# Attention scores of a two-layer diffusion step as sums of three fp32r products, in twelve steps of two heads

## The chip, the core and the metric

The kernel runs on one core of a Trainium2 chip. The metric is the device time of one execution in microseconds (us). The core has a matrix engine (TensorE, PE in the rows, with its weight loads shown apart as PEld), a vector engine (VectorE, DVE), a scalar engine (ScalarE, ACT), GpSimd (POOL) and SyncE (SP), which here only issues DMAs. Each engine works through its own list of instructions in a fixed order and waits on semaphores for the others.

## The reference, cut to what matters

128 context tokens and 256 latent tokens go through two layers of width 1024. A layer is a half-step SwiGLU, a token mixing, and another half-step SwiGLU, each with a norm ahead and behind and modulated by a condition. The mixing projects once and splits the columns among four groups: A (a short gated convolution), B (differential attention), C (a convolution of width 31) and D (grouped-query attention, GQA).

```
def diff_attention(q, k, v, lam):          # 4 heads, 2 maps each, q and k of width 32
        s = jnp.einsum("bqhmd,bshmd->bhmqs", qb, k).astype(jnp.float32) * scale
        p = jax.nn.softmax(s, axis=-1)
        w = p[:, :, 0] - lam * p[:, :, 1]
        return jnp.einsum("bhqs,bshd->bqhd", w.astype(v.dtype), v)
def gqa_attention(q, k, v):                # 4 heads on 2 key heads, width 64
        s = jnp.einsum("bqkgd,bskd->bkgqs", qb, k).astype(jnp.float32) * scale
        p = jax.nn.softmax(s, axis=-1)
        return jnp.einsum("bkgqs,bskd->bqkgd", p.astype(v.dtype), v)
```

Latent tokens attend to 128 cached keys and to the 256 latent ones (384 keys), context tokens to themselves (128 keys). Queries come in three tiles of 128 tokens: t = 0 and 1 latent, t = 2 context. A score product is thus 128 queries by 384 or 128 keys.

## The kernel before, in words

All tokens (3 tiles of 128) stay in SBUF and the weights stream through once. `W` (class at the top) keeps the stream: L156 loads a tile `st` of 128x1024 fp32 on SP's queue, L167 (ACT) casts it to its high half in fp32r, L168 (DVE) subtracts to get the low half; the pair is `wu`. Every large product is a sum of three fp32r products, high·high, high·low and low·high (L542 to L544, L548 to L550 and L576 to L578). Only the small attention products are still plain fp32 matmuls, which the array runs as two passes.

`mix` is the token mixing of one layer. Ahead of the attention it projects group C and D; group C's 31-tap convolution is a chain of 62 multiply-adds on DVE (`conv_some`, L799, tile `cacc`), dealt out a few at a time between other work. Then come 24 attention steps: twelve GQA heads (three query tiles by four heads), then twelve heads of differential attention. Each step is three functions, run one loop pass apart: `first` makes the scores (`probs`: L871 matmul into a PSUM bank `ps_s`, L872 DVE row maximum, L876 ACT exp into `p` with its sum), `second` transposes p (L886) and copies it to `wt` (L888), `third` multiplies with the values (L894, `ps_pv`). A differential head has two maps, joined on DVE (L954, L956, L960). After four heads DVE scales the result into `mo` (L931 or L979). The queries and keys, transposed, lie in `qTd`, `kTd`, `kTdp` (differential) and `qTg`, `kTg`, `kTgp` (GQA), as fp32.

Between the steps run the `fills`, the other projections of the mixing: in the GQA steps `qk_fill` and `v_fill` (for the differential attention, L542 to L544), in the differential steps twelve `a_fill` (group A, L548 to L550, 24 products each) and `norm_fill` (group C's norm, after the convolution). Behind the loop the output projection `ps_o` (L576 to L578) starts with the parts that are done.

The loop, which sets the order of the code:

```
            for i in range(n + 2):
                if i < n:
                    units[i][0]()
                todo = flush()
                run(fills[i])
                run(todo)
                if 1 <= i <= n:
                    units[i - 1][1]()
                if i >= 2:
                    units[i - 2][2]()
                W.tick()
                conv_some(CONV1)
```

`later(f, n)` puts a function off by n passes; `flush` returns those that are due. A scheduler then arranges the instructions of each engine, starting from this order, so an engine's list is near to it but not equal. PSUM has six banks for the large results (`bank`: `ps_j`, `ps_s`, `ps_pv`, `ps_o`) and two for small ones (`mbank`: transposes).

## Time and profile before

| what | value |
|---|---|
| median of 3 runs | 1563.77 us (1561.25 to 1564.76) |
| the profiled execution | 1562.17 us, its span 1560.4 us |
| mean granted TensorE clock | 0.986 of full speed |
| PE busy | 1500.0 us, 96% of the span |
| DVE busy | 1050.7 us, 67% |
| ACT busy | 633.7 us, 41% |
| attention steps, layer 0 | 373.6 to 475.4 us: GQA 51.5 us, differential 50.3 us |
| attention steps, layer 1 | 1130.9 to 1229.8 us: GQA 50.1 us, differential 48.8 us |

Busy shares are means over stages with different limits. PE is busy nearly all the time, but a busy PE may be running small products, or at a lower clock; the granted clock is told per stretch, as a share of full speed. The two attention stretches of a layer are cut where the first score product, the first product of group A and the first product of the output projection start.

### The profile page before, as it was taken

What the parts mean: (1) busy time and instruction counts of PE and PEld (TensorE: products, weight loads), DVE (VectorE), ACT (ScalarE), POOL (GpSimd) and SP (SyncE); (2) the same over time, 40 slices, a digit from 0 to 9 for tenths busy, and PEclk for the clock granted to TensorE, in tenths of its full rate; (3) what the DMA queues carried; (4) which work ended last, traced back from release to release, by engine and by line L of the source; (5) the groups of instructions that cost most, each with busy time, mean ns of one, the idle gap of its engine ahead of it and who ended that gap; (6) DMA issues with size and microseconds to landing.
All of it is one profiled execution on the core that took longest, in us unless ns stands there. A gap on an engine that the chain in (4) does not pass through costs nothing. (4 is left out here: it accounts for less than half of the span.)

```text
span 1560.4 us, 20661 instructions
## 1 busy us (share of the span) xinstructions
PE 1500.0 (96%) x7924; PEld 1319.9 (85%) x7924; DVE 1050.7 (67%) x1454; ACT 633.7 (41%) x1103; POOL 126.4 (8%) x234
## 2 busy tenths in 40 slices
PE   6899999999999999999999999999999999999997
PEld 3699998776887899998879999887768879999885
DVE  3678879867887845677586766984788796333432
ACT  3442233263466632334263333434545764323331
POOL 1101000021001201000021000002100120000000
PEclk9999999998999999999999999999999999999998
DMA  8668767733224555675546656773322245444431
GB/s 307 227 222 261 236 211 236 245 109 98 68 70 145 150 177 179 212 233 172 189 150 215 206 188 200 231 234 110 112 73 92 72 160 175 134 132 138 135 122 41
DMA packets 73619, 260.13 MB, mean 167 GB/s; under 512 B 9728, under 2 KB 9856, under 8 KB 73520
## 3 DMA queue, kind: packets, MB, share of 16 engines
q1 hardware_dynamic: 68112, 246.32, 48.5%
q0 software_dynamic: 4976, 11.70, 2.7%
q8 instruction: 62, 1.02, 0.3%
q10 hardware_dynamic: 432, 0.79, 0.1%
q14 instruction: 37, 0.30, 0.1%
HBM read 256.36 MB, written 2.41 MB: 166 GB/s over the span
## 5 line engine op out<-in xcount | busy, mean ns | idle before, releaser
L168 DVE TENSOR_TENSOR wu<-st,wu 128x1024 fp32r<-128x1024 f32 x322 | 391.6, 1219 | 296.5 <-ACT wu L167 295.9
L167 ACT CAST wu<-st 128x1024 fp32r<-128x1024 f32 x322 | 337.0, 1050 | 585.4 <-DMA st<-ws 253.7
L549 PE MATMUL ps_f<-h,wu 128*128 128x384 f32 x1248 | 418.6, 335 | 0.0
L548 PE MATMUL ps_f<-h,wu 128*128 128x384 f32 x1248 | 418.4, 336 | 0.0
L550 PE MATMUL ps_f<-h,wu 128*128 128x384 f32 x1248 | 418.3, 335 | 0.0
L279 DVE SCALAR_TENSOR_TENSOR acc<-ast,sc,acc 128x1024 f32<-128x1024 f32 x224 | 281.6, 1281 | 27.5 <-DMA ast<-w_ada 26.9
L548 PEld LDWEIGHTS ps_f<-h,wu 128*128 128x128 f32 x1248 | 234.9, 188 | 7.8 <-issue 4.2
L550 PEld LDWEIGHTS ps_f<-h,wu 128*128 128x128 f32 x1248 | 235.0, 188 | 0.0
L549 PEld LDWEIGHTS ps_f<-h,wu 128*128 128x128 f32 x1248 | 235.0, 188 | 0.0
L576 PE MATMUL ps_o<-wu,hid_s 128*128 128x512 f32 x528 | 206.5, 391 | 0.0
L577 PE MATMUL ps_o<-wu,hid_s 128*128 128x512 f32 x528 | 206.0, 390 | 0.0
L578 PE MATMUL ps_o<-wu,hid_s 128*128 128x512 f32 x528 | 205.5, 389 | 0.0
L576 PEld LDWEIGHTS ps_o<-wu,hid_s 128*128 128x128 f32 x528 | 99.1, 188 | 26.1 <-issue 5.9
L578 PEld LDWEIGHTS ps_o<-wu,hid_s 128*128 128x128 f32 x528 | 99.1, 188 | 20.6
L577 PEld LDWEIGHTS ps_o<-wu,hid_s 128*128 128x128 f32 x528 | 99.1, 188 | 20.0
L543 PE MATMUL ps_j<-wu,h 128*128 128x512 f32 (+1 forms) x192 | 73.1, 381 | 5.3 <-DVE wu L168 5.3
L542 PE MATMUL ps_j<-wu,h 128*128 128x512 f32 (+1 forms) x192 | 74.5, 388 | 0.0
L544 PE MATMUL ps_j<-wu,h 128*128 128x512 f32 (+1 forms) x192 | 72.6, 378 | 0.0
L676 ACT ACTIVATE sg<-ps_f 128x384 f32<-128x384 f32 x78 | 38.0, 487 | 83.4 <-PE ps_f L550 79.3
L799 DVE SCALAR_TENSOR_TENSOR cacc<-upad,late,cacc 128x399 f32<-128x399 f32 x120 | 69.9, 630 | 0.0
L337 POOL DMA_DIRECT2D gd<-grow x24 | 11.7, 496 | 676.0 <-DVE grow L329 676.0
L677 DVE TENSOR_TENSOR hid<-sg,ps_f 128x384 f32<-128x384 f32 x78 | 42.9, 549 | 23.3 <-PE ps_f L550 23.3
(234 smaller groups left out, 1701.0 us busy)
## 6 DMA issues: line engine op xcount, KB each, us to landing
st<-ws SPq DMA_DIRECT2D x320, 512.0 KB, 3.9
ast<-w_ada SPq DMA_DIRECT2D x128, 512.0 KB, 4.4
a<-ada SPq DMA_DIRECT2D x16, 512.0 KB, 9.3
G<-gd POOLq DMA_DIRECT2D x12, 512.0 KB, 4.7
brow<-b_ada POOLq DMA_DIRECT2D x24, 64.0 KB, 5.6
prow<-norm_post POOLq DMA_DIRECT2D x24, 64.0 KB, 6.1
x<-x_sample SPq DMA_DIRECT2D x2, 512.0 KB, 5.2
x<-x_prompt SPq DMA_DIRECT2D x1, 512.0 KB, 8.9
```

What stands on the lines that cost most here:

```text
L167: nc.scalar.copy(out=u[:, 0, :], in_=x)
L168: nc.vector.tensor_tensor(out=u[:, 1, :], in0=x, in1=u[:, 0, :].bitcast(F32), op=ALU.subtract)
L279: nc.vector.scalar_tensor_tensor(out=self.acc[c], in0=w, scalar=s1, in1=self.acc[c], op0=ALU.mult, op1=ALU.add)
L542: nc.tensor.matmul(out, lhsT=hk(h, k, 0, tsl), rhs=wh, start=start, stop=False)
L543: nc.tensor.matmul(out, lhsT=hk(h, k, 0, tsl), rhs=wl, start=False, stop=False)
L544: nc.tensor.matmul(out, lhsT=hk(h, k, 1, tsl), rhs=wh, start=False, stop=stop)
L548: nc.tensor.matmul(out, lhsT=wh, rhs=hk(h, k, 0, sl), start=start, stop=False)
L549: nc.tensor.matmul(out, lhsT=wh, rhs=hk(h, k, 1, sl), start=False, stop=False)
L550: nc.tensor.matmul(out, lhsT=wl, rhs=hk(h, k, 0, sl), start=False, stop=stop)
L576: nc.tensor.matmul(out, lhsT=pr[:, 0, s, tsl], rhs=u[:, 0, hsl], start=(q == 0), stop=False)
L577: nc.tensor.matmul(out, lhsT=pr[:, 0, s, tsl], rhs=u[:, 1, hsl], start=False, stop=False)
L578: nc.tensor.matmul(out, lhsT=pr[:, 1, s, tsl], rhs=u[:, 0, hsl], start=False, stop=(q == n - 1))
```

## The change: what it does

1. **Scores as three fp32r products.** The tiles of queries and keys become fp32r with a high and a low half. A helper `halves` writes the high half on ACT (the scaled copy that was there before) and the low half on DVE (one scalar_tensor_tensor, new). The cached keys come in one DMA into `kc` and pass through `halves` too. `probs` gets a list of maps and makes high·high, high·low and low·high of all of them in turn, each map in its own bank.
2. **Twelve steps a layer, of two heads.** A GQA step has two maps, in rows 0 to 63 and 64 to 127 of the array; a differential step has four maps, in four groups of 32 rows.
3. **The order around the steps.** All lags are one pass; in a pass the first fill runs, then `third` of two steps back, then what was put off, then the other fills, then `second`. Weight ticks (two) and convolution taps (8 for 4) per pass are doubled, `a_fill`s come two per step from step 6, `norm_fill`s at steps 8, 9 and 10.
4. **Room.** p gets 6 buffers for 4, `mo` one for 2, the convolution tiles (`c3`) 3 for 4 with `upad` and `zT` sharing a place of their own. `norm_fill` keeps its transposed result in SBUF rather than in three large banks, and the silu at the end is two instructions of 384 rather than six of 128. The tiles `ast` for the condition's weights move from a pool of the whole kernel into each SwiGLU; `sink` and `sc` shrink, `grow` is written in place.

```
-QK_LAG = 2
+QK_LAG = 1
-MIX_LAG = 3
-NORM_LAG = 2
-NORM_AT = 16
-NORM_GAP = 2
+MIX_LAG = 1
+NORM_LAG = 1
+NORM_AT = 8
-CONV1 = 4
-A_STEPS = 11
+CONV1 = 8
...
-        with tc.tile_pool(name=nm("fp"), bufs=1) as fp:
+        with tc.tile_pool(name=nm("fp"), bufs=1) as fp, tc.tile_pool(name=nm("adap"), bufs=2) as ap_:
...
+            kc = mp.tile([P, TOK], F32, tag="p", name=nm("kc"), bufs=6)
+            nc.gpsimd.dma_start(out=kc.rearrange("p (c n) -> p c n", c=3), in_=a["cache_kT"][l])
+
+            def halves(hi, lo, src, scale=1.0):
+                nc.scalar.mul(hi, src, scale)
+                nc.vector.scalar_tensor_tensor(
+                    out=lo, in0=src, scalar=scale, in1=hi.bitcast(F32), op0=ALU.mult, op1=ALU.subtract
+                )
...
-            def probs(t, st, idx, lhsT, rhs):
+            def probs(t, st, maps):
                 nk = TOK if t < 2 else P
-                ps = bank(nm("ps_s"))
-                nc.tensor.matmul(ps[:, 0:nk], lhsT=lhsT, rhs=rhs, start=True, stop=True)
-                nc.vector.tensor_reduce(
...
+                pss = [bank(nm("ps_s")) for _ in maps]
+                for a_, b_ in ((0, 0), (0, 1), (1, 0)):
+                    for ps, (idx, lhsT, rhs) in zip(pss, maps):
+                        nc.tensor.matmul(
+                            ps[:, 0:nk], lhsT=lhsT(a_), rhs=rhs(b_), start=(a_ + b_ == 0), stop=(a_ == 1)
+                        )
+                res = []
+                for ps, (idx, lhsT, rhs) in zip(pss, maps):
+                    nc.vector.tensor_reduce(
...
-                mo = mp.tile([P, 256], F32, tag="mo", name=nm("mo"), bufs=2)
+                mo = mp.tile([P, 256], F32, tag="mo", name=nm("mo"))
...
-                nc.scalar.mul(qTd[:, :, t * P : (t + 1) * P], pq[:, 0:2, :], 32 ** -0.5)
-                nc.scalar.copy(out=kTd[:, :, (t + 1) * P : (t + 2) * P] if t < 2 else kTdp, in_=pq[:, 2:4, :])
+                halves(qTd[:, 0, :, tsl], qTd[:, 1, :, tsl], pq[:, 0:2, :], 32 ** -0.5)
+                k0, k1 = (kTd[:, s, :, ksl] if t < 2 else kTdp[:, s] for s in range(2))
+                halves(k0, k1, pq[:, 2:4, :])
...
-                for hd in range(4)
+                for c in range(2)
...
-                fills[12 + (j * A_STEPS) // 12].append(f)
-            fills[12 + A_STEPS].append(a_split)
+                fills[6 + j // 2].append(f)
+            fills[n].append(a_split)
...
-                run(fills[i])
+                run(fills[i][:1])
+                if i >= 2:
+                    units[i - 2][2]()
                 run(todo)
+                run(fills[i][1:])
                 if 1 <= i <= n:
                     units[i - 1][1]()
-                if i >= 2:
-                    units[i - 2][2]()
-                W.tick()
+                for _ in range(2):
+                    W.tick()
                 conv_some(CONV1)
```

In the lists of the engines this looks as follows (layer 0). The helper lines shift with the edit: L168 of before is L166 of the change, L548 to L550 are L546 to L548, L799 is L803, L871 is L884, L872 is L889, L886 is L904, L894 is L912, L931 is L959; L712 is the low half in `halves`.

PE in the differential half of before: the scores of one head's two maps stand between the products with the values and group A's products.

```order
L886 MATMUL ps_pT_3841<-early,p_3749 128x128 x3
L894 MATMUL ps_pv_3700<-Vd_2812,wt_3804 128x64 x3
L871 MATMUL ps_s_3862<-kTd_2806,qTd_2808 128x384
L871 MATMUL ps_s_3867<-kTd_2806,qTd_2808 128x384
L548 MATMUL ps_j_3828<-h_2555,wu_3495 128x384
L549 MATMUL ps_j_3828<-h_2555,wu_3495 128x384
```

PE at the same place of the changed kernel: twelve score products of four maps stand together, and the products of one map are kept apart by those of the others.

```order
L904 MATMUL ps_pT_3765<-early,p_3623 128x128 x3
L884 MATMUL ps_s_3772<-kTd_2807,qTd_2809 128x384
L884 MATMUL ps_s_3773<-kTd_2807,qTd_2809 128x384
L884 MATMUL ps_s_3774<-kTd_2807,qTd_2809 128x384
L884 MATMUL ps_s_3772<-kTd_2807,qTd_2809 128x384
L884 MATMUL ps_s_3773<-kTd_2807,qTd_2809 128x384
L884 MATMUL ps_s_3775<-kTd_2807,qTd_2809 128x384
L884 MATMUL ps_s_3774<-kTd_2807,qTd_2809 128x384
L884 MATMUL ps_s_3775<-kTd_2807,qTd_2809 128x384
L884 MATMUL ps_s_3772<-kTd_2807,qTd_2809 128x384
L884 MATMUL ps_s_3773<-kTd_2807,qTd_2809 128x384
L884 MATMUL ps_s_3774<-kTd_2807,qTd_2809 128x384
```

PE of the changed kernel at the seam of the two halves, in its first differential step: here the block is broken up by transposes and by the last GQA products with the values (`ps_pv_3482`), and the fourth map `ps_s_3603` stands last, right ahead of group A's products.

```order
L884 MATMUL ps_s_3602<-kTd_2807,qTd_2809 128x384
L904 MATMUL ps_pT_3509<-early,p_3359 128x128 x3
L912 MATMUL ps_pv_3482<-Vg_2815,wt_3507 128x64 x3
L904 MATMUL ps_pT_3583<-early,p_3451 128x128
L912 MATMUL ps_pv_3482<-Vg_2815,wt_3513 128x64 x3
L904 MATMUL ps_pT_3587<-early,p_3454 128x128
L884 MATMUL ps_s_3603<-kTd_2807,qTd_2809 128x384 x3
L546 MATMUL ps_j_3636<-h_2553,wu_3270 128x384
```

DVE of before late in the GQA half: four convolution taps, a row maximum, a weight's low half, and so on.

```order
L799 SCALAR_TENSOR_TENSOR cacc_2936<-upad_2820,late,cacc_2936 128x399 x4
L872 TENSOR_REDUCE st_3418<-ps_s_3419 128x1
L465 TENSOR_TENSOR mTd_3111<-ps_mo_3424,mTd_3111 128x2x128
L168 TENSOR_TENSOR wu_3445<-st_3233,wu_3445 128x1024
L799 SCALAR_TENSOR_TENSOR cacc_2936<-upad_2820,late,cacc_2936 128x399 x4
L872 TENSOR_REDUCE st_3418<-ps_s_3454 128x1
```

DVE of the changed kernel from there to the seam: eight taps stand ahead of a pair of row maxima, the low halves of queries and keys are new, and the row maxima of the first differential step stand behind `mo_3581` and seven more taps.

```order
L803 SCALAR_TENSOR_TENSOR cacc_2937<-upad_2821,late,cacc_2937 128x399 x8
L889 TENSOR_REDUCE st_3441<-ps_s_3442 128x1
L889 TENSOR_REDUCE st_3441<-ps_s_3443 128x1
L712 SCALAR_TENSOR_TENSOR qTd_2809<-ps_qk_3489,qTd_2809 128x2x128
...
L803 SCALAR_TENSOR_TENSOR cacc_2937<-upad_2821,late,cacc_2937 128x399
L959 TENSOR_TENSOR mo_3581<-ps_pv_3482,st_3283 128x256
L803 SCALAR_TENSOR_TENSOR cacc_2937<-upad_2821,late,cacc_2937 128x399 x7
L889 TENSOR_REDUCE st_3599<-ps_s_3600 128x1
```

## Rows read from the trace of the kernel before

**Rows 1.** The page's first lines: the span, and busy time, share of the span and count of instructions of each engine.

```profile
span 1560.4 us, 20661 instructions
PE 1500.0 (96%) x7924; PEld 1319.9 (85%) x7924; DVE 1050.7 (67%) x1454; ACT 633.7 (41%) x1103; POOL 126.4 (8%) x234
```

**Rows 2.** Busy time of each engine (us, with the count) by stretch: the GQA and the differential half of layer 0, then of layer 1. Columns: stretch, its length, PE, PEld, DVE, ACT, POOL, granted clock, DMA share, GB/s.

```profile
373.60:425.10 51.50, 48.88 (x254) 36.98 (x253) 42.23 (x78) 21.97 (x53) 3.54 (x5) 0.90 0.24 78
425.10:475.40 50.30, 49.10 (x290) 41.97 (x289) 39.84 (x103) 31.52 (x81) 5.09 (x10) 0.97 0.21 69
1130.90:1181.00 50.10, 47.46 (x254) 35.97 (x253) 42.18 (x78) 21.93 (x53) 3.54 (x5) 0.93 0.24 81
1181.00:1229.80 48.80, 47.60 (x290) 40.49 (x289) 39.78 (x103) 31.52 (x81) 5.11 (x10) 1.00 0.22 71
```

**Rows 3.** PE's timeline around single score blocks (start us, duration us, then line, operation, tiles; x4 are two maps of two passes each): one of 384 keys in GQA; then of the differential half one in which the maps ran one behind the other in part, one that is split in two, a common one of 384 keys with what stands around it, and one of 128 keys.

```profile
395.64 0.91 PE L871 MATMUL ps_s<-kTg,qTg 64*128 64x384 f32 x2
396.48 0.50 PE L542 MATMUL ps_j<-wu,h 128*128 128x512 f32 x1
...
431.52 1.16 PE L871 MATMUL ps_s<-kTd,qTd 32*128 32x384 f32 x4
...
443.97 0.91 PE L871 MATMUL ps_s<-kTd,qTd 32*128 32x384 f32 x2
...
445.62 0.91 PE L871 MATMUL ps_s<-kTd,qTd 32*128 32x384 f32 x2
...
449.37 0.78 PE L894 MATMUL ps_pv<-Vd,wt 128*128 128x64 f32 x6
450.08 0.91 PE L871 MATMUL ps_s<-kTd,qTd 32*128 32x384 f32 x4
450.93 0.45 PE L548 MATMUL ps_j<-h,wu 128*128 128x384 f32 x1
451.21 0.34 PE L549 MATMUL ps_j<-h,wu 128*128 128x384 f32 x1
451.39 0.35 PE L550 MATMUL ps_j<-h,wu 128*128 128x384 f32 x1
451.57 0.34 PE L548 MATMUL ps_j<-h,wu 128*128 128x384 f32 x1
...
467.98 0.49 PE L871 MATMUL ps_s<-kTdp,qTd 32*128 32x128 f32 x4
468.39 0.45 PE L548 MATMUL ps_j<-h,wu 128*128 128x384 f32 x1
```

**Rows 4.** The same timeline in the first SwiGLU: four fp32 products of 512 columns (eight passes) in four groups of 32 columns of the array, and the product behind them.

```profile
116.90 1.06 PE L291 MATMUL ps_ada<-acc,ones 128*32 128x512 f32 x8
117.90 0.45 PE L548 MATMUL ps_f<-h,wu 128*128 128x384 f32 x1
```

**Rows 5.** DVE's groups by line and shape in the GQA half of layer 0 (373.6 to 425.1 us): count, busy us and mean ns, idle time before them and what ended it.

```profile
L799 DVE SCALAR_TENSOR_TENSOR cacc<-upad,late,cacc 128x399 f32<-128x399 f32 x41 | 23.6, 630 | 0.0
L168 DVE TENSOR_TENSOR wu<-st,wu 128x1024 fp32r<-128x1024 f32 x8 | 9.7, 1219 | 2.8 <-ACT wu L167 2.8
L872 DVE TENSOR_REDUCE st<-ps_s 128x1 f32<-128x384 f32 x8 | 4.4, 554 | 2.6 <-PE ps_s L871 2.6
L872 DVE TENSOR_REDUCE st<-ps_s 128x1 f32<-128x128 f32 x3 | 0.9, 290 | 0.8 <-PE ps_s L871 0.8
...
L820 DVE TENSOR_TENSOR dn<-ps_j,rstd 128x256 f32<-128x256 f32 x1 | 0.4, 424 | 1.5 <-POOL rstd L460 1.5
```

**Rows 6.** The same view of the differential half of layer 0 (425.1 to 475.4 us), four of its groups.

```profile
L872 DVE TENSOR_REDUCE st<-ps_s 128x1 f32<-128x384 f32 x16 | 8.5, 545 | 0.9 <-PE ps_s L871 0.9
L960 DVE SCALAR_TENSOR_TENSOR p<-p,nb,p 128x384 f32<-128x384 f32 x8 | 4.9, 612 | 0.0
L954 DVE RECIPROCAL st<-st 128x2 f32<-128x2 f32 x11 | 1.8, 161 | 3.3 <-ACT p L876 3.3
L960 DVE SCALAR_TENSOR_TENSOR p<-p,nb,p 128x128 f32<-128x128 f32 x2 | 0.7, 345 | 0.0
```

**Rows 7.** PE's waits from the first score product of layer 0 to the end of group C's product (373.6 to 493 us): what waited for what, us in total, times, longest.

```profile
PE ps_j L543 <- DVE wu L168: 2.6, 1, 2.6
PE ps_mo L903 <- DVE mo L994: 0.9, 1, 0.9
...
PE ps_pv L894 <- ACT wt L888: 0.6, 1, 0.6
PE ps_j L548 <- ACT p L876: 0.6, 1, 0.6
```

**Rows 8.** Two views of one place, PE's timeline at the first of these waits and then the busy times by stretches of 3 us (columns as in rows 2).

```profile
375.29 0.40 PE L542 MATMUL ps_j<-wu,h 128*128 128x512 f32 x1
378.30 0.80 PE L543 MATMUL ps_j<-wu,h 128*128 128x512 f32 x1 [2.62 <-DVE wu L168]
...
376.00:379.00 3.00, 0.70 (x2) 0.60 (x3) 3.00 (x6) 0.00 (x0) 0.62 (x1) 0.78 0.06 22
379.00:382.00 3.00, 3.00 (x7) 1.40 (x5) 3.00 (x7) 0.67 (x2) 0.00 (x0) 0.50 0.79 255
...
385.00:388.00 3.00, 3.00 (x10) 2.28 (x9) 2.67 (x5) 0.31 (x1) 0.00 (x0) 0.51 0.51 142
388.00:391.00 3.00, 3.00 (x22) 2.21 (x20) 1.54 (x2) 2.44 (x9) 0.00 (x0) 1.00 0.11 38
```

More of the change, by code (lines that the diff above doesn't have):

```diff
@@ L264, in __init__, with step @@
             self.k = 0
-        def step(self, pool):
+        def step(self, pool, ap_):
             k = self.k
@@ L656, in more @@
                     rate[0] -= 1
-                    if f.step(fp):
+                    if f.step(fp, ap_):
                         done.append(f)
@@ L802, in conv_some @@
                         )
+            halves(kTd[:, 0, :, 0:P], kTd[:, 1, :, 0:P], kc[:, 0:256].rearrange("p (c n) -> p c n", c=2))
+            halves(kTg[:, 0, 0:P], kTg[:, 1, 0:P], kc[:, 256:384])
             def d_rows(t, ps):
@@ L848, in d_tail @@
                 nc.tensor.transpose(pt[:, 256:384], dn[:, 256:384], ident)
-                nc.scalar.mul(
-                    qTg[:, :, t * P : (t + 1) * P], pt[:, 0:256].rearrange("p (g n) -> p g n", g=2), 64 ** -0.5
-                )
-                nc.scalar.copy(out=kTg[:, (t + 1) * P : (t + 2) * P] if t < 2 else kTgp, in_=pt[:, 256:384])
+                tsl, ksl = slice(t * P, (t + 1) * P), slice((t + 1) * P, (t + 2) * P)
+                halves(
+                    qTg[:, 0, :, tsl], qTg[:, 1, :, tsl], pt[:, 0:256].rearrange("p (g n) -> p g n", g=2),
+                    64 ** -0.5,
+                )
+                k0, k1 = (kTg[:, s, ksl] if t < 2 else kTgp[:, s, :] for s in range(2))
+                halves(k0, k1, pt[:, 256:384])
             us = W.take(4)
@@ new lines, in first @@
+                    pm = probs(
+                        t, st,
+                        [
+                            (
+                                4 * c + j, lambda s, j=j: qTd[32 * j : 32 * j + 32, s, c, tsl],
+                                lambda s, j=j: kt[32 * j : 32 * j + 32, s, c, :],
+                            )
+                            for j in range(4)
+                        ],
+                    )
+                    box[c] = []
+                    for j in range(2):
+                        i0 = 4 * c + 2 * j
+                        p0, p1 = pm[2 * j : 2 * j + 2]
+                        nc.vector.reciprocal(out=st[:, 2, i0 : i0 + 2], in_=st[:, 1, i0 : i0 + 2])
+                        nb = sm.tile([P, 1], F32, tag="nb", name=nm("nb"))
+                        nc.vector.scalar_tensor_tensor(
+                            out=nb, in0=st[:, 1, i0 : i0 + 1], scalar=lam[:, 4 + l : 5 + l],
+                            in1=st[:, 2, i0 + 1 : i0 + 2], op0=ALU.mult, op1=ALU.mult,
+                        )
+                        nc.vector.scalar_tensor_tensor(
+                            out=p0[:, 0:nk], in0=p1[:, 0:nk], scalar=nb, in1=p0[:, 0:nk],
+                            op0=ALU.mult, op1=ALU.add,
+                        )
+                        box[c].append(p0)
@@ L1131, in mix @@
                 for box in [{}]
-                for hd in range(4)
+                for c in range(2)
             ]
-            fills = [[] for _ in range(len(units) + 2)]
+            n = len(units)
+            fills = [[] for _ in range(n + 2)]
             early = [lambda t=t, p=p: qk_fill(t, p) for t in range(NT) for p in range(2)]
```

152 lines of the change are left out of this document (75 added, 77 removed).

## Prediction

> **What bounds the kernel now.** I read the page's totals first: PE is busy 96% of the span, DVE 67%, ACT 41% [rows 1]. A shorter piece of PE work is therefore worth its time wherever DVE keeps up, and the question is whether it does in the stretches that the change touches. The view by stretch answers it [rows 2]. Each layer has a GQA half (51.5 and 50.1 us) and a differential half (50.3 and 48.8 us). In the differential halves PE is busy all but 1.2 us and DVE only 39.8 us: PE is the bound there. In the GQA halves PE stands idle about 2.6 us and has a clock below full (0.90 and 0.93), while DVE is busy 42.2 us.
>
> The timeline of layer 0 shows why the clock is low [rows 8]. PE waited 2.62 us for a weight's low half, which DVE made late; behind that wait the granted clock is 0.50, the lower of the two levels (1.2 rather than 2.4 GHz), until about 388 us. From the shares in these rows: 1.3 us of the stretch 376 to 379 and nearly all of 379 to 388, some 10.2 us, in which half the time, 5.1 us, is lost. So the GQA half is one in which DVE is late, not one in which PE has too much to do. The differential half, which holds two waits of 0.6 us [rows 7], has a clock of 0.97 [rows 2]: shorter waits cost less or nothing of it.
>
> **What a score block costs before.** A block is what PE does for the scores of one step. One map of 384 keys in GQA takes 0.84 us from its first product to the next instruction (395.64 to 396.48), and two maps of the differential half take 0.85 us (450.08 to 450.93), the same: in different rows of the array two products run in the time of one. With 128 keys it is 0.41 us [rows 3]. Two passes of 384 columns and two of 128 differ by 0.44 us, which is 0.86 ns a column: a pass of 384 columns is 0.33 us, and 0.19 us a block is left for changing over. The product behind starts its successor 0.28 us later rather than the 0.18 us that follow (450.93, 451.21, 451.39), so 0.10 us more belongs to each block. The differential half has eight blocks of 384 keys and four of 128 (eleven heads; one is split in two, 443.97 and 445.62). That is 8 x 0.95 + 4 x 0.51 = 9.6 us, and 0.25 to 0.3 us each for two blocks in which the maps ran partly in turn (1.16 us in place of 0.91, [rows 3]): 10.2 us.
>
> **What it costs after.** An fp32r product of 384 columns follows the last one after 0.18 us [rows 3], so three of them are 0.54 us where the two fp32 passes were 0.66. If the maps of a step run side by side, a block is 0.19 + 0.54 + 0.10 = 0.83 us, for four maps. With 128 keys I take a load and a product at what the products with the values show, six in 0.71 us (449.37 to 450.08), 0.118 us each: 0.19 + 3 x 0.118 + 0.10 = 0.64 us. The differential half keeps three blocks of 384 and two of 128 (the first differential step stands ahead of it). The order lists show four of the blocks broken by transposes or products with the values; each break costs the changeover again, 0.29 us. Sum: 2.5 + 1.3 + 1.2 = 5.0 us, **5.2 us less PE work** in each differential half.
>
> Whether four maps run side by side, no row shows directly. The nearest are two row groups (above) and four column groups: eight passes of 512 columns done in 1.0 us [rows 4], where eight in turn at 0.86 ns a column would take 3.5 us. I take side by side. The Trainium skill ("TensorE: Matmul & The Clock Gate", Part 3, the table of measured speedups) gives 3.07 times for four row groups rather than 4. By it the products of a block would take 0.70 us, not 0.54, which is 0.5 us more over three blocks and about 1 us in the whole sum.
>
> **What is added.** The low halves are DVE work. Ten of them fall in the GQA half, eight of 256 columns and two of 128. A DVE operation of this size from PSUM takes 0.424 us (L820, [rows 5]); the same form of instruction takes 0.612 us at 384 columns and 0.345 at 128 [rows 6], so 0.48 at 256. That makes 8 x 0.424 + 2 x 0.29 = 4.0 us at least and 8 x 0.48 + 2 x 0.345 = 4.5 at most. I take 4.2, so DVE has 46.4 us to do in 51.5. Its waits there were 9.3 us, of which [rows 5] name 2.8 (a cast that was late), 3.4 (scores that were not there), 1.5 (the norm's root on POOL) and, in smaller groups, 1.6. The second kind should shrink: PE's blocks in this half drop too, and a pair of maxima waits once where two waited twice. With 1 us of it left, 46.4 + 2.8 + 1.5 + 1.0 = 51.7 us; if the late cast goes as well, 48.9. Before was 51.5 and 50.1, so I cost this half at **nothing**, with both ends kept: 0.2 slower to 2.6 faster in layer 0, to 1.2 faster in layer 1. PE's saving there is hidden behind DVE and worth nothing.
>
> The high halves are the scaled copies that ACT made before. Taps, casts, maxima and exps are as many as before, in pairs. The differential half gets no new DVE work, but DVE's 39.8 us must now fit in some 45, and its chain (four maxima, four exps, then L954 waiting for ACT, 3.3 us before, [rows 6]) is longer per step. I let this eat 0.2 of the 5.2. The moves of room (`ast`, one `mo`, the silu) I cost at nothing: DVE and ACT have a third and more of the span free [rows 1]. If that cover fails, a wait as long as the attention's longest, 2.6 us [rows 7], is what I would expect of it, and a gain of as much if a wait is moved away.
>
> **Sum.** Twice 5.0 us less, against the profiled execution: 1562.17 - 10 = 1552.2 us. That execution lies 1.6 us under the median of the runs shown, so on the median 1563.8 - 10 = 1553.8, **1554 us**.
>
> **Rivals.**
> *DVE binds both halves.* Speaks for it: after the change DVE's share in the differential half is 39.8 of 45, with waits for ACT, POOL and PE of some 10 us before that would have to shrink by half. Against it: these waits lie in a stretch where PE was the bound, and waits of an engine that isn't the bound are slack. Where the waits stay, 39.8 + 9 = 48.8 us is left of 50.3, and the time is 1561 to 1563 us, no change. The Trainium skill ("TensorEngine Tiling (Array Packing)", PSUM Bottleneck) says that tiling speeds up TensorE but not what empties PSUM, which may then be the bound. The rows agree as far as they go: the maxima cost 0.545 us a map whatever the array does.
>
> *The maps don't run side by side*, so the change doesn't do what it says. If each load and product takes its own 0.118 us, twelve take 1.42 and a block 1.71 us: 5 x 1.71 + 1.2 = 9.7 us, only 0.5 less than before. Time: 1562.8 us. Wholly in turn, 12 x 0.18 + 0.29 = 2.45 us for 384 keys: 3 x 2.45 + 2 x 1.71 + 1.2 = 12 us, 1.8 us slower a layer, 1567 us.
>
> *Slower: a wait at the seam and a clock at half.* The last map of the first differential step stands behind the GQA products with the values and needs a PSUM bank. Four maps want four of the six banks, and the one of `ps_pv` comes free when DVE has made `mo`, behind its taps. DVE is the late engine in that half; behind eight taps (8 x 0.63 = 5.0 us, [rows 5]) PE could wait as it does at 378 us. The price is that of rows 8: 2.6 us and 5.1 us of lost clock, 7.7 us in a half that PE bounds. Less the 5.0 gained that is 2.7 us slower a layer, 1569 us. It decides from a wait between the 0.6 us beside which the clock kept 0.97 and the 2.6 us behind which it fell to 0.50. Against it: the wait of 2.62 us of before need not come again where the order is another, and PE can be late in a half that DVE bounds at no cost.
>
> *More is gained.* The late low half doesn't come again, the clock stays up, and the GQA half follows its lower end (2.6 and 1.2 us): 1550 us. With DVE's waits at half in both halves, 3.5 us more: 1546.5 us.
>
> **How the numbers follow.** The sum 0.46; more 0.12; DVE binds both halves 0.17; not side by side 0.08; slower at the seam 0.17. A measurement of this kernel can tell about 0.2%, 3.1 us. The sum's own range is 1550 to 1559. "Faster" takes the sum, "more" and some parts of DVE's case and the third: 0.64. "Same" takes the rest of DVE's case and most of the third, 0.18; "slower" the seam and the wholly serial case, 0.18. The range runs from 1546.5, the end of "more", to 1564.5, which takes in DVE's case and the pairs at 0.118 us; what lies above it is the seam.
>
> **What would show it.** Right: blocks of twelve products in about 0.8 us from the first to the next instruction; the differential halves at about 45 us with PE busy nearly throughout; the GQA halves at 49 to 52 us with DVE busy 46. Wrong: score products of one block that start 0.118 us or more apart without overlap; differential halves still near 50 us, with PE waiting for `p` or `wt` (DVE binds); a wait of PE for `mo` or a bank ahead of the first group A product with a clock of 0.50 behind it (the seam); or a difference that lies outside the two attention stretches, in the SwiGLU or the start, where I see none.

## The result: slower by 0.7%

The changed kernel takes 1575.8 us (median of 5 runs, 1570.61 to 1577.4), the kernel before 1564.76 us beside it: ratio 1.0070, 95% interval 1.0049 to 1.0091. I had forecast 1554 us and a gain.

The page's first lines of the changed kernel, which answer to [rows 1]:

```profile
span 1575.6 us, 20887 instructions
PE 1494.9 (95%) x7996; PEld 1321.4 (84%) x7996; DVE 1061.4 (67%) x1483; ACT 622.7 (40%) x1093; POOL 129.4 (8%) x232
```

PE has 5 us less to do and the span is 15 us longer. Busy time by stretch (columns as in [rows 2]): layer 0 from the first mixing projection to the first score, from there to group A's first product, and from there to the first output projection; then the last two for layer 1:

```profile
332.60:382.20 49.60, 42.73 (x194) 33.13 (x192) 36.27 (x70) 25.84 (x59) 12.14 (x18) 0.98 0.33 110
382.20:429.80 47.60, 43.77 (x263) 35.56 (x262) 43.50 (x85) 23.17 (x56) 1.08 (x2) 0.86 0.27 88
429.80:479.80 50.00, 46.69 (x309) 41.80 (x308) 40.33 (x107) 26.58 (x77) 7.05 (x10) 0.95 0.20 68
1145.40:1192.20 46.80, 43.31 (x264) 35.16 (x263) 42.88 (x84) 23.56 (x56) 1.08 (x2) 0.86 0.28 91
1192.20:1241.60 49.40, 45.99 (x309) 41.18 (x309) 41.16 (x108) 26.56 (x77) 7.05 (x10) 0.96 0.21 70
```

The differential halves did not shrink (50.0 and 49.4 us, after 50.3 and 48.8), though PE has 2.4 and 1.6 us less to do there. PE idles 3.3 and 3.4 us in them, where it idled 1.2 us in each. The clock is 0.86 in the GQA half, where it was 0.90 and 0.93. Since the scores start later in the order, the fair comparison takes projections and GQA half as one stretch. The table is worked out from the traces, each row between the same products of PE in every kernel; a kernel's column ends at its own profiled span. (Names of the other columns: below.)

```
us of the stretch                 before after  b2    b4    a8    a9    b6    a11
start to first mixing projection  331.2  332.6 331.9 332.0 332.2 334.7 329.6 332.0
  to group A's first product       93.9   97.3  94.7 101.8  95.8  91.9  90.3  88.7
  to the first output projection   50.3   50.0  53.0  52.1  49.7  48.6  51.9  47.7
  to the last one                  40.7   41.0  40.8  42.5  41.0  41.1  41.8  41.4
  to the SwiGLU's first ps_f       15.0   17.4  16.7  14.4  15.5  15.5  14.4  17.4
  to layer 1's mixing projection  556.8  558.2 558.5 556.7 556.9 557.0 556.7 558.3
  to group A's first product       93.0   95.7  93.5  99.0  95.8  92.2  90.6  90.4
  to the first output projection   48.8   49.4  51.4  52.1  49.3  48.3  53.4  48.9
  to the last one                  40.7   42.9  40.8  39.6  42.9  41.2  40.3  42.7
  to the SwiGLU's first ps_f       15.1   16.2  16.7  15.5  14.4  15.5  15.5  16.2
  to the end                      274.8  274.8 275.3 274.6 274.6 274.6 274.6 274.8
```

The loss has two main places: about 3 us a layer ahead of group A, and about 6 us in stretches that I had not looked at: the start, the norms between mixing and SwiGLU (17.4 and 16.2 us after 15.0) and the stage borders within the 558 us. Another 2.2 us lie in layer 1's output projection (42.9 us after 40.7), which I did not follow.

**Ahead of group A: one wait longer, two new ones.** PE's waits from the first score of layer 0 to the first output projection (as in [rows 7]); the two score waits (L884) are the seam:

```profile
PE ps_s L884 <- ACT p L893: 2.2, 1, 2.2
PE ps_s L884 <- ACT Vdp L1077: 1.5, 1, 1.5
PE ps_z L1162 <- DVE z L1152: 1.1, 1, 1.1
PE ps_pT L904 <- ACT wt L906: 1.0, 3, 0.4
```

The wait of [rows 8] stands right ahead of this stretch and has grown from 2.62 to 3.88 us. Its chain, from the timelines of ACT, DVE and PE:

```profile
369.94 0.38 ACT L711 ACTIVATE qTg<-ps_dT 128x256 fp32r<-128x256 f32 x1
374.49 0.28 ACT L711 ACTIVATE kTg<-ps_dT 128x128 fp32r<-128x128 f32 x1 [4.18 <-DVE qTg L712]
374.66 0.48 ACT L814 ACTIVATE sqd<-ps_j 128x384 f32<-128x384 f32 x1
...
374.04 0.42 DVE L712 SCALAR_TENSOR_TENSOR qTg<-ps_dT,qTg 128x256 fp32r<-128x256 f32 x1
378.74 0.42 DVE L827 TENSOR_TENSOR dn<-ps_j,rstd 128x256 f32<-128x256 f32 x1 [1.52 <-POOL rstd L458]
379.81 1.22 DVE L166 TENSOR_TENSOR wu<-st,wu 128x1024 fp32r<-128x1024 f32 x1
...
381.08 0.80 PE L541 MATMUL ps_j<-wu,h 128*128 128x512 f32 x1 [3.88 <-DVE wu L166]
```

ACT makes the high half of the queries, and then waits 4.18 us before it may make that of the keys, until DVE has read the same PSUM tile for the queries' low half. The squares for the norm (`sqd`) are queued behind it on ACT, the norm's root behind those, `dn` behind the root, and the weight's low half that PE wants behind `dn`.

At the seam, the timelines of PE, DVE and ACT:

```profile
420.06 1.15 PE L884 MATMUL ps_s<-kTd,qTd 32*128 32x384 f32 x6 [1.52 <-ACT Vdp L1077]
428.59 1.32 PE L884 MATMUL ps_s<-kTd,qTd 32*128 32x384 f32 x3 [2.23 <-ACT p L893]
...
418.69 1.05 ACT L165 CAST wu<-st 128x1024 fp32r<-128x1024 f32 x1 [1.67 <-DMA st<-ws]
419.64 0.37 ACT L1077 COPY Vdp<-ps_j 128x256 f32<-128x256 f32 x1
...
422.50 4.45 DVE L803 SCALAR_TENSOR_TENSOR cacc<-upad,late,cacc 128x399 f32<-128x399 f32 x8
426.86 0.48 DVE L889 TENSOR_REDUCE st<-ps_s 128x1 f32<-128x128 f32 x2
...
428.07 0.37 ACT L893 ACTIVATE p<-ps_s,st 128x128 f32<-128x128 f32 x1
```

and the busy times there in stretches of 2 us (columns as in [rows 2]):

```profile
418.00:420.00 2.00, 0.54 (x5) 0.34 (x3) 2.00 (x6) 1.31 (x3) 0.00 (x0) 1.00 0.01 4
...
422.00:424.00 2.00, 2.00 (x10) 1.57 (x10) 2.00 (x4) 0.72 (x2) 0.00 (x0) 0.50 0.78 302
...
432.00:434.00 2.00, 2.00 (x9) 2.00 (x7) 1.96 (x5) 0.00 (x0) 0.00 (x0) 0.50 0.00 0
```

The first wait, 1.52 us, ends with ACT's copy `Vdp` of a value projection. That copy stands on ACT behind a weight's cast, which waited 1.67 us for its DMA; the taps are not in this chain. The bank that PE wants for the fourth map, the second wait, is held by an earlier map of 128 keys: its row maximum stands on DVE behind eight taps (422.50 to 426.86), its exp behind the maximum. PE idles in both, and the clock stands at 0.50 from about 421.4 to 435.1 us, 13.7 us, two fifths of it in the differential half.

**Around the norms: one more filler a turn.** DVE's timeline from one tile's `xn` to the next one's, between mixing and SwiGLU of layer 0; first before, then after the change:

```profile
517.64 0.75 DVE L491 TENSOR_SCALAR xn<-x,rstd 128x1024 f32<-128x1024 f32 x1 [0.84 <-POOL rstd L479]
...
520.15 1.41 DVE L534 SCALAR_TENSOR_TENSOR x<-yg,rstd,x 128x512 f32<-128x512 f32 x2
521.47 1.22 DVE L168 TENSOR_TENSOR wu<-st,wu 128x1024 fp32r<-128x1024 f32 x1
522.61 1.43 DVE L465 TENSOR_TENSOR h<-hf,h 128x256 fp32r<-128x256 f32 x4
523.95 1.22 DVE L168 TENSOR_TENSOR wu<-st,wu 128x1024 fp32r<-128x1024 f32 x1
526.01 0.75 DVE L491 TENSOR_SCALAR xn<-x,rstd 128x1024 f32<-128x1024 f32 x1 [0.85 <-POOL rstd L479]
```

```profile
514.28 0.75 DVE L489 TENSOR_SCALAR xn<-x,rstd 128x1024 f32<-128x1024 f32 x1 [0.86 <-POOL rstd L477]
...
516.78 1.41 DVE L532 SCALAR_TENSOR_TENSOR x<-yg,rstd,x 128x512 f32<-128x512 f32 x2
518.10 1.28 DVE L278 SCALAR_TENSOR_TENSOR acc<-ast,sc,acc 128x1024 f32<-128x1024 f32 x1
519.30 1.43 DVE L463 TENSOR_TENSOR h<-hf,h 128x256 fp32r<-128x256 f32 x4
520.64 1.28 DVE L278 SCALAR_TENSOR_TENSOR acc<-ast,sc,acc 128x1024 f32<-128x1024 f32 x1
521.84 1.22 DVE L166 TENSOR_TENSOR wu<-st,wu 128x1024 fp32r<-128x1024 f32 x1
523.91 0.75 DVE L489 TENSOR_SCALAR xn<-x,rstd 128x1024 f32<-128x1024 f32 x1 [0.85 <-POOL rstd L477]
```

A filler is work that the scheduler puts between the norm's own instructions: a weight's low half (`wu`) or an accumulation for the condition (`acc`). Two fillers stood in a turn of 8.4 us before (8.5 us in the stage's first turn, from 509.2 us), three stand in one of 9.6 us now, and DVE idles only 0.85 us in either. The order lists show the added filler in seven of the ten turns that stand at the kernel's stage borders, and the traces of the two kernels show seven as well.

### The profile page after: what moved, and what is told of

The parts are those of the page before. It is cut to its first block, busy times and chain, and to the rows that moved or that the text cites. A ratio compares the mean times of both kernels' runs of the same rounds, so it can differ in the third digit from the quotient of the medians.

```text
span 1575.6 us, 20887 instructions
## 1 busy us (share of the span) xinstructions
PE 1494.9 (95%) x7996; PEld 1321.4 (84%) x7996; DVE 1061.4 (67%) x1483; ACT 622.7 (40%) x1093; POOL 129.4 (8%) x232
## 5 line engine op out<-in xcount | busy, mean ns | idle before, releaser
L166 DVE TENSOR_TENSOR wu<-st,wu 128x1024 fp32r<-128x1024 f32 x322 | 391.8, 1219 | 295.4 <-ACT wu L165 294.3
L548 PE MATMUL ps_f<-h,wu 128*128 128x384 f32 x1248 | 418.4, 335 | 0.0
L546 PE MATMUL ps_f<-h,wu 128*128 128x384 f32 x1248 | 417.5, 335 | 0.0
L546 PEld LDWEIGHTS ps_f<-h,wu 128*128 128x128 f32 x1248 | 234.7, 188 | 7.8 <-DVE hid L675 4.2
L548 PEld LDWEIGHTS ps_f<-h,wu 128*128 128x128 f32 x1248 | 234.8, 188 | 0.0
L803 DVE SCALAR_TENSOR_TENSOR cacc<-upad,late,cacc 128x399 f32<-128x399 f32 x120 | 69.0, 629 | 0.0
L335 POOL DMA_DIRECT2D gd<-prow x24 | 11.8, 497 | 672.0 <-DVE prow L327 672.0
L675 DVE TENSOR_TENSOR hid<-sg,ps_f 128x384 f32<-128x384 f32 x78 | 42.9, 550 | 31.2 <-PE ps_f L548 31.2
```

Of the source, the lines that this page charges most:

```text
L166: nc.vector.tensor_tensor(out=u[:, 1, :], in0=x, in1=u[:, 0, :].bitcast(F32), op=ALU.subtract)
L546: nc.tensor.matmul(out, lhsT=wh, rhs=hk(h, k, 0, sl), start=start, stop=False)
L548: nc.tensor.matmul(out, lhsT=wl, rhs=hk(h, k, 0, sl), start=False, stop=stop)
```

## Experiments

All ratios are to the kernel before, run beside it on the same chip. Worked out from the intervals, the difference of two rows is good to 0.2 or 0.3%.

```
                                              ratio  95% interval
after     the change                          1.0070 1.0049 1.0091
a1        high halves first                   1.0042 1.0028 1.0057
a2        taps in two lots                    1.0033 1.0008 1.0058
a7        both                                1.0020 1.0009 1.0032
a8        full sink                           1.0036 1.0022 1.0050
a9        high halves first, two lots, sink   0.9981 0.9969 0.9993
a4        fp32 scores in two-head steps       0.9989 0.9972 1.0006
a11       low halves left out                 0.9979 0.9962 0.9996
b1        before, weights' pool moved         0.9986 0.9969 1.0003
b2        before, sink halved                 1.0082 1.0065 1.0099
b4        before, split scores                1.0101 1.0081 1.0122
b5        b4, high halves first               1.0071 1.0050 1.0092
b6        b4, low halves left out             0.9984 0.9971 0.9996
a12       a4, full sink, two lots             0.9970 0.9958 0.9982
a14       a12, weights' pool at the top       0.9999 0.9985 1.0012
a15       a14, taps in one lot                0.9982 0.9966 0.9998
```

**a1, a2, a7: the turn-taking and the seam.** a1 makes both high halves before the low ones, by a `part` of `halves` that is 1 for the high half on ACT and 2 for the low half on DVE. The place for the differential attention (that for GQA has the same edit):

```
-                halves(qTd[:, 0, :, tsl], qTd[:, 1, :, tsl], pq[:, 0:2, :], 32 ** -0.5)
...
-                halves(k0, k1, pq[:, 2:4, :])
+                for part in (1, 2):
+                    halves(qTd[:, 0, :, tsl], qTd[:, 1, :, tsl], pq[:, 0:2, :], 32 ** -0.5, part)
+                    halves(k0, k1, pq[:, 2:4, :], 1.0, part)
```

> The changed kernel with one edit: for each tile ACT writes both high halves (queries, then keys) before DVE makes both low halves; in the changed kernel ACT's high half of the keys waits for DVE's low half of the queries, 4.2 and 5.4 us at the start of the attention. Theory A (this turn-taking holds up ACT, and with it the norm and the weight's low half that PE waits 3.9 us for): ACT's waits for L712 vanish, the 3.9 us wait of layer 0 falls to 2.6 us or less, the stretch from the first mixing projection to the first product of group A (97.2 us) falls by 1.5 to 4 us, and the whole by 3 to 8 us, to 1568 to 1573 us. Theory B (the loss sits at the seam and in the clock behind it): that stretch changes by less than 1 us and the whole stays at 1574 to 1577 us.

Ratio 1.0042, 0.28% better than the change; the stretch is 94.4 us after 97.3. Theory A holds, but the gain is partly passed on: PE now waits 3.8 us in all, once, for the keys' low half itself (a score product waits for L714), which DVE makes late. The seam's two waits are shorter in this run as well (1.6 and 0.5 us for 2.2 and 1.5), so it does not part theory A from theory B cleanly.

a2 deals the taps out in two lots:

```
                 run(fills[i][:1])
+                conv_some(CONV1 // 2)
...
-                conv_some(CONV1)
+                conv_some(CONV1 // 2)
```

> The changed kernel with its eight convolution taps a pass dealt out in two lots of four, one behind the first fill and one at the end of the pass. Theory B (at the seam PE waits for banks that come free only behind eight taps on DVE): the two waits of score products at the seam, 1.5 and 2.2 us in layer 0, fall to under 2 us together, the clock stays up or falls for less than the 13.7 us of now, and the whole gains 4 to 10 us, to 1566 to 1572 us. Theory A (turn-taking of ACT and DVE at the start of the attention): under 2 us gained, 1574 to 1577 us.

Ratio 1.0033. PE's waits at the seam of this kernel:

```profile
PE ps_s L884 <- ACT p L893: 1.8, 1, 1.8
PE ps_pT L904 <- ACT wt L906: 1.4, 2, 0.7
PE ps_s L884 <- ACT Vdp L1077: 0.3, 1, 0.3
```

and its busy times there in stretches of 4 us:

```profile
426.00:430.00 4.00, 2.19 (x17) 1.80 (x16) 4.00 (x10) 3.05 (x9) 0.00 (x0) 1.00 0.48 174
430.00:434.00 4.00, 4.00 (x15) 3.87 (x14) 4.00 (x10) 0.22 (x1) 0.00 (x0) 0.57 0.02 4
434.00:438.00 4.00, 4.00 (x31) 3.67 (x30) 2.83 (x8) 3.13 (x11) 0.00 (x0) 1.00 0.00 0
```

The two score waits are 2.1 us in place of 3.7 (two waits for `wt`, 1.4 us, are new at this place), the half clock lasts some 3.4 us in place of 13.7, and the differential halves are 46.8 and 47.1 us. Theory B holds too; its expected time (1566 to 1572 us) and theory A's (1568 to 1573 us) were both met. Together:

> The changed kernel with high halves first and taps in two lots of four, `sink` still halved. If the gains of the parts add (after 1.0070, less 0.0028 and 0.0037): 1.0005, and the step to the kernel with the full `sink` (0.9981) is 0.0024. If both edits remove the same wait: 1.003 to 1.004.

Ratio 1.0020; adding would have given 1.0005, removing the same wait 1.003 to 1.004. It lies between, and the interval does not settle it.

**b1, b2, a8: the room.** b1 moves the pool of the condition's weights in the kernel before:

```
-    ap_ = ctx.enter_context(tc.tile_pool(name="adap", bufs=2))
...
+        with tc.tile_pool(name=nm("fp"), bufs=1) as fp, tc.tile_pool(name=nm("adap"), bufs=2) as ap_:
```

> The kernel before with one part of the change: the pool of the tiles for the condition's weights moves from the whole kernel into each SwiGLU, so that its first load waits for the room of the mixing. Theory E (this moves one more accumulation on DVE, 1.28 us, into each turn of the norms between mixing and SwiGLU, which after the change take 9.6 us a tile in place of 8.4): the stretch from the last output projection of the mixing to the SwiGLU's first large product grows from 15.1 to 16.5 to 17.5 us in both layers, and the whole by 2 to 6 us, to 1567 to 1571 us. Rival (the move is hidden): 1563 to 1566 us.

Ratio 0.9986, no loss: theory E falls, and the stretches around the norms stay at 15.1 and 15.0 us. So the added filler has another cause. b2 halves `sink`:

```
-    sink = cp.tile([P, D], BF16, name="sink")
+    sink = cp.tile([P, 512], BF16, name="sink")
...
-                out=sink[:, hsl], in_=x[t][:, hsl], func=AF.Square, scale=D ** -0.5,
+                out=sink, in_=x[t][:, hsl], func=AF.Square, scale=D ** -0.5,
...
```

> The kernel before with one small part of the change: the scrap tile `sink`, into which ACT writes squares that nobody reads, is halved, so that both halves of a row write the same place. In the lists of DVE each turn of the norms between two tiles then holds one more filler (a weight's low half, 1.22 us), as it does in the changed kernel and not before. Theory F (this costs a filler in each such turn, six stages with two to three turns each): the stretch from mixing to SwiGLU grows from 15.1 to 16.2 to 17.5 us, that from the SwiGLU of layer 0 to the mixing of layer 1 (556.8 us) by 1 to 2 us, the start by about 1 us, and the whole by 5 to 8 us, to 1569 to 1572 us. Rival (DVE has the time): under 1.5 us, 1563 to 1565 us.

Ratio 1.0082, more than the whole change, and above the 5 to 8 us that I expected. Of the profiled execution's 13 us, the rows of the table for the start, around the norms and for the stage borders take 6.3; 2.7 and 2.6 us lie in the differential halves, where no instruction touches `sink`. In layer 0 PE waits 1.7 us there for a `wt` (0.6 before) and the clock is at half for 3.4 us more. Whether that belongs to `sink` is open: b1, which loses nothing, has 51.9 and 50.3 us in these halves too. a8 gives the change its old `sink` (for room, three buffers for four of the small columns):

```
-    sm = ctx.enter_context(tc.tile_pool(name="sm", bufs=4))
+    sm = ctx.enter_context(tc.tile_pool(name="sm", bufs=3))
-    sink = cp.tile([P, 512], BF16, name="sink")
+    sink = cp.tile([P, D], BF16, name="sink")
...
```

> The changed kernel with `sink` at its old size (and three buffers for four of the small column tiles, to make room). Theory F (the halved scrap tile is half of the loss): the stretch from mixing to SwiGLU falls from 17.4 and 16.2 to 15.1 us, the one behind it by 1 to 1.5 us, and the whole by 4 to 7 us, to 1568 to 1572 us; the two halves of the attention stay as they are, 97 and 50 us. Rival: the attention alone is the loss, 1574 to 1577 us.

Ratio 1.0036; in DVE's order the third filler of a turn is gone, and the turn shown above takes 8.5 us (512.16 to 520.65):

```profile
512.16 0.75 DVE L489 TENSOR_SCALAR xn<-x,rstd 128x1024 f32<-128x1024 f32 x1 [0.86 <-POOL rstd L477]
515.99 1.28 DVE L278 SCALAR_TENSOR_TENSOR acc<-ast,sc,acc 128x1024 f32<-128x1024 f32 x1
518.53 1.28 DVE L278 SCALAR_TENSOR_TENSOR acc<-ast,sc,acc 128x1024 f32<-128x1024 f32 x1
520.65 0.75 DVE L489 TENSOR_SCALAR xn<-x,rstd 128x1024 f32<-128x1024 f32 x1 [0.85 <-POOL rstd L477]
```

The halved scrap tile is half of the change's loss, about 5 us; a9 against a7 below, which differ by the same edits, gives 0.39%. The two squares of a row, which wrote different halves, now write the same place; that the scheduler then counts on a later `xn` and puts one more filler ahead of it is argued from the lists, not shown.

**b4, b5, b6, a4, a11: what the split costs.** b4 puts the split scores into the kernel before, with its 24 steps and its order; for room it also has the pool of b1 and `grow` written in place:

```
-                nc.tensor.matmul(ps[:, 0:nk], lhsT=lhsT, rhs=rhs, start=True, stop=True)
+                for a_, b_ in ((0, 0), (0, 1), (1, 0)):
+                    nc.tensor.matmul(
+                        ps[:, 0:nk], lhsT=lhsT(a_), rhs=rhs(b_), start=(a_ + b_ == 0), stop=(a_ == 1)
+                    )
```

and queries and keys through `halves`, as in the change.

> The kernel before, with its 24 steps and its order, and only the first part of the change: queries and keys in high and low halves, scores as three fp32r products (one map a block, or two in a differential head), `sink` at full size; for room the condition's weights have their pool in each SwiGLU and `grow` is written in place. A block gets 0.12 us shorter (0.54 for 0.66 us), 2.5 us a layer; the low halves put 4.2 us a layer on DVE in the GQA half and make ACT take turns with it. Theory C (the low halves and the turn-taking are the loss of the attention): the stretch to the first product of group A grows from 93.9 to 96 to 99 us, and the whole to 1567 to 1574 us. Theory D (the steps of two heads are the loss): 1560 to 1565 us.

Ratio 1.0101, the slowest of all and slower than I expected even by theory C: 101.8 and 99.0 us to group A, and ACT's waits for the queries' low half are there again (4.39 and 5.93 us at 373 and 380 us). b5 is b4 with a1's edit:

> The kernel before with split scores in its 24 steps (1.0101 to before), and both high halves made on ACT ahead of the low halves on DVE. Theory A (ACT's turn-taking with DVE is a large part of the 16 us): 1.004 to 1.0075, the stretch to the first product of group A 96 to 99 us rather than 101.8. Theory C1 (DVE's work on the low halves alone is): 1.0085 to 1.0105.

Ratio 1.0071: turn-taking is 0.3% of the 1.0, as in the change, though the two intervals overlap a little. In the profiled executions the stretch to group A is shorter in layer 0 alone (95.3 us for 101.8, then 99.7 for 99.0). b6 is b4 without the low halves on DVE, the three products being made of high halves (`lhsT(0)`, `rhs(0)`):

> The same 24 steps with three products of high halves and the low halves left out. Theory C (low halves and turn-taking are the whole loss of the split): 0.997 to 1.001, with 92 to 94 us to the first product of group A. Theory G (three products a block cost by themselves, in single steps): 1.004 to 1.01.

Ratio 0.9984: the products cost nothing. That they gain is not shown, since the pool that b6 shares with b1 gives 0.9986 by itself. The rest of the split's cost comes with the low halves on DVE. In the steps of two heads it is the same. a11, the change with three products of high halves:

> The changed kernel with the three products of each map made of high halves alone: the low halves are left out on DVE, the count of score products stays. Theory C (the low halves on DVE are what the GQA half pays): as with single fp32 products, the stretch to the first product of group A is 90 to 91 us and the whole 1560 to 1564 us. Theory G (three products for four maps, which hold four banks, are the cost): 94 to 97 us there and 1570 to 1576 us.

Ratio 0.9979 and 88.7 us to group A, 0.91% better than the change. a4, the change with one fp32 product a map (`for a_, b_ in ((0, 0),)`, fp32 tiles, no low halves):

> The changed kernel with the scores as single fp32 products again, in the same twelve steps of two heads; the low halves of queries and keys, and the products with them, are left out. Four maps side by side take two passes of 384 columns, 0.66 us, where three fp32r products take 0.54, so a block costs 0.12 us more, 1 us a layer. Theory C (the low halves on DVE, 4.2 us a layer, and what they hold up are the loss of the GQA half): the stretch up to the first product of group A falls by 3 to 6 us a layer and the whole to 1564 to 1570 us. Theory D (the steps of two heads and their order are the loss, whatever the products are): under 3 us gained, 1573 to 1577 us.

Ratio 0.9989, a little faster than theory C had it, and not told apart from a11. What one sees in both is the low halves' absence; one or three products make no difference that these runs can tell.

**a9, a12, a14, a15: versions that are faster.** a9 has the edits of a1, a2 and a8.

> The changed kernel with three edits together: both high halves ahead of the low halves, the taps in two lots of four, and `sink` at its old size (with three buffers for the small columns). If the three gains add (4.4, 5.8 and 5 us by ratio): 1559 to 1563 us, a little under the kernel before. If the first two remove the same waits: 1563 to 1567 us.

Ratio 0.9981: the change with its three side effects removed is 0.2% faster than the kernel before, and the first case was right. Against a7 the full `sink` gives 0.39%. All the low halves are still in a9, and yet it is as fast as a11, which leaves them out but keeps the lot of eight taps and the halved `sink`: what the low halves cost hangs on the order around them. a12 is a4 with a2's edit and the full `sink`:

> The changed kernel's steps of two heads with what the runs so far speak for: single fp32 score products, no low halves, taps in two lots of four, `sink` at full size. If the gains found one by one add (0.9989 with single products, then 0.0034 for the scrap tile and 0.0037 for the taps): ratio 0.991 to 0.993, 1549 to 1553 us. If the taps' gain was the low halves' in another form: 0.994 to 0.997, 1554 to 1559 us.

Ratio 0.9970, the best found, and the second case: the gains don't add without the low halves. Against a9 it is 0.11% faster, within the intervals: with the order mended, single fp32 products without low halves gain nothing that these runs can tell. Its first 335.6 us are 4 us longer than those of before. a14 puts the weights' pool back at the top:

> The last kernel (steps of two heads, single fp32 products, taps in two lots, `sink` at full size) with the pool of the condition's weights back at the top, as before the change. Theory H (that pool's move costs the first SwiGLU: PE waits 5.6 to 8.3 us for rows at about 157 us where it waited 2.0): the stretch up to the first mixing projection falls from 335.6 to 331 to 332.5 us, and the ratio from 0.997 to 0.994 to 0.9955, 1555 to 1558 us. Rival (the start differs from run to run, and what the pool loses there it gains at the wait for the first `sg`): 0.9965 to 0.9985.

Ratio 0.9999, slower than theory H and its rival both said, and 0.29% slower than a12, with intervals that do not meet. The start is 334.0 us and theory H is not borne out; the start varies from 329.5 to 336.4 us over all profiled kernels with the pool in the SwiGLU. a15 has the taps in one lot again:

> The same with the taps in one lot of eight as in the changed kernel. If the lot of eight delays row maxima only where DVE is loaded with low halves: the same time as with two lots, within 0.1%. If it is the seam's cost in any case, as with the low halves (0.37%): 0.2 to 0.4% slower than with two lots.

Ratio 0.9982: not slower than two lots, by this pair rather 0.17% faster, with intervals that overlap. The lot of eight cost 0.37% where DVE is loaded with low halves (a2); without them no cost is seen. Among a4, a12, a14 and a15 the intervals reach from 0.9958 to 1.0012, and I don't rank them further.

## Why the prediction was wrong, point by point

**The blocks: side by side, but not the 5 us a half.** Four maps do run side by side. PE's timeline of the changed kernel around its second and third differential step:

```profile
437.36 0.44 PE L884 MATMUL ps_s<-kTd,qTd 32*128 32x384 f32 x2
437.73 0.33 PE L904 MATMUL ps_pT<-early,p 128*128 128x128 f32 x1
437.99 0.79 PE L884 MATMUL ps_s<-kTd,qTd 32*128 32x384 f32 x10
438.71 0.44 PE L546 MATMUL ps_j<-h,wu 128*128 128x384 f32 x1
...
444.20 1.76 PE L884 MATMUL ps_s<-kTd,qTd 32*128 32x384 f32 x12
445.89 0.44 PE L546 MATMUL ps_j<-h,wu 128*128 128x384 f32 x1
```

Ten products take 0.72 us; at 0.118 us each they would take 1.18, in turn 1.8. The rival "not side by side" falls. But the next block takes 1.69 us, its products starting in groups (the list holds two maps back behind the others). With breaks and waits the score blocks of this half come to 6.4 us from first product to next instruction, and with 0.10 us for each of nine pieces to 7.3, where I had 5.0: PE saved 2.9 us of the 10.2, not 5.2. Of the step of four maps I had counted the banks only at the seam. By the rows above PE's busy time in the halves fell by 2.4 and 1.6 us; a lower clock (0.95 and 0.96 after 0.97 and 1.00) took back some 1 and 2 us of what the blocks saved. And I had let DVE's longer chain eat 0.2 us of it, while PE's idle time there rose by 2.1 and 2.2 us, in waits such as those for `z` and `wt`. That is part of what the rival "DVE binds both halves" said. So the main term of the forecast, twice 5.0 us less, came out as -0.3 and +0.6 us.

A gain is there all the same: between b4 and a8, which both split the scores with a full `sink`, the steps of two heads, with the order and the room that come with them, are worth 1.0101 to 1.0036, 10 us. That this is the size of my sum is luck. By the table 9.2 us of it lie ahead of group A, where I had nothing, and 5.2 in the differential halves, where I had all ten; other stretches give 2 back. With fp32 scores, and pool and `sink` as before, the same steps give only 0.0 and 0.2% (a14 and a15). Over all profiles the differential halves take 46.8 to 50.0 us in steps of two heads and 48.8 to 53.4 us in single ones, by the means about 3 us a half.

**The seam: the rival that I gave 0.17 came true in part.** It had the right place and the right kind: score products waiting for banks, and the clock at half behind it. Waits of 1.5 and 2.2 us, a half clock of about 13.7 us in layer 0 (2.6 and 10.2 us had been the price). Only the second wait stands behind eight taps, and its bank was that of an earlier map; the first bank was that of a value projection, late by a DMA; neither was that of `ps_pv`. One reading ahead of it was wrong: the 0.97 of layer 0's differential half in [rows 2] does not come from the two waits of 0.6 us. The clock was at 0.50 for 3.4 us from 425.5 us on, at this same seam, with no wait of PE recorded from 405 us on. So a wait is not all that the clock fell behind here, and the change adds some 10 us of half clock at the seam, not 13.7. Most of the slow stretch lies in the GQA half, so the differential halves changed by -0.3 and +0.6 us, not by +2.7.

**The GQA half: the step that failed.** I costed it at nothing, from 4.2 us more DVE work against waits that I expected to shrink. DVE's work was about as said. Before, the stretch ahead of the GQA half read:

```profile
331.20:373.60 42.40, 40.50 (x188) 31.94 (x186) 31.28 (x60) 24.74 (x58) 9.32 (x15) 1.00 0.38 126
```

DVE has 36.3 + 43.5 = 79.8 us in projections and GQA half together, by the rows above, where it had 31.3 + 42.2 = 73.5; the low halves took 0.42 and 0.28 us each, twelve of them in this stretch 4.6 us, the lower end of my bound with two that I had not counted. But my sum let 2.4 us of DVE's waits for scores and all of its 1.6 us of small waits go, and gave an upper end for layer 0 alone (51.7 us would be 1.6 us slower in layer 1). And PE's wait for the weight's low half grew where I expected it to stay or go. "The high halves are the scaled copies that ACT made before" was true of their number and wrong of their place in the queue: the second of a pair now waits for DVE (4.18 us in the rows above), with the norm's squares behind it. I had put no wait into `halves` at all. Price by a1 and b5: 0.3%, 5 us. The larger part comes with the low halves and what stands behind them on DVE: 0.87% by b5 against b6, 0.63% by a11 against the change less the turn-taking, 10 to 14 us where I had nothing to 1 us. It is not the price of DVE's busy time as such, which is 4.6 us a layer, and it overlaps with the seam's: a9 has the same low halves and is as fast as a11.

**The moves of room: costed at nothing, worth 5 us.** I took DVE's 67% of the whole span as cover. The stretch decides: in a norm's turn DVE idles 0.85 of 8.4 us. The bound of 2.6 us that I gave was too small, the part I named (the weights' pool) was harmless by itself (b1), and `sink` I had not looked at. The order lists had the added filler before any run.

**In sum,** from before to the change over b4 and a8: +1.01% for the split (turn-taking 0.30, low halves 0.87, and -0.16 for products and room, which is no more than b1's pool), -0.65% for the steps of two heads with their order, +0.34% for the scrap tile. Each part is good to 0.2 or 0.3%, and another order of taking them would share them out differently. DVE as the bound of the GQA half was right, and so "slower" came from work added to the engine that was late, which I had let be hidden by slack that wasn't there.

## What to carry to other kernels

When an operation is split over two engines that read the same tile in PSUM, count whom the second one waits for and what is queued behind it; making all of one engine's reads first took 0.3% off the time here. A tile that saves room can change the order of an engine's instructions: compare the engines' lists at every stage, also far from the edit, and price a filler by the idle time of that stage, not of the span. Where an engine is late, put no long lot of fillers ahead of what gives back a bank that the next step needs.

## What was not expected of the hardware

ACT's read of a PSUM tile stood behind DVE's earlier read of another part of the same tile in the four cases read here, at the start of layer 0's attention (4.18 and 5.39 us of waiting in the change, 4.39 and 5.93 in b4), though neither writes it. The trace ends each wait by a semaphore of DVE's instruction, so the wait is in the program; whether the chip asks for it was not tried. And products of four maps in four row groups ran side by side: ten score products of 384 columns took 0.72 us, the time of four in turn, and in a9 a block of twelve took 0.73 us (440.61 to 441.34).
